# The last expert of a mixture of experts: its order of work and the split of its last columns

## The chip, the core and the metric

The kernel runs on one core of a Trainium2 chip. The metric is the device time of one execution in microseconds (us). The engines are TensorE (PE in the rows, PEld its weight loads), VectorE (DVE), ScalarE (ACT), GpSimd (POOL) and SyncE (SP). Each works through its own instructions in program order; they meet through semaphores. Weights come from HBM by DMA, issued from SP.

## What is computed

Two transformer blocks run over 256 tokens of width 1024. The change lies in the last part of the second block, a mixture of 32 experts with top-4 routing, and in the final norm behind it:

```python
def expert_block(args):
    xb, e = args
    u = xb @ w1[e] + b1[e]                                  # first product
    glu = jnp.minimum(u[:, ::2], SWIGLU_LIMIT)
    lin = jnp.clip(u[:, 1::2], -SWIGLU_LIMIT, SWIGLU_LIMIT)
    a = glu * jax.nn.sigmoid(SWIGLU_ALPHA * glu) * (lin + 1.0)
    return a @ w2[e] + b2[e]                                # second product
...
y = jnp.zeros((T + 1, D), jnp.float32).at[row_tok].add(yb * row_gate[:, None])
...
x = x + gt_f[:, None, :] * moe(...)
return rms_norm(x, g_final)
```

`w1[e]` is 1024 x 2048 and `w2[e]` 1024 x 1024, all in float32.

## The kernel before

**Dense dispatch.** Every expert has room for 64 tokens. Expert e gathers its tokens by a matmul with a one-hot matrix (`xe`), and its result goes back to the 256 tokens, weighted by the gates, by a matmul with another one-hot matrix (`gT`). Tokens beyond 64 for one expert are treated by the loop under `tc.If(items > 0)` at the end.

**The stream of weights.** `seq` lists the weight tiles in the order in which they are loaded and used. Each is 1 MB (128 x 2048 floats). `(1, e, k)`, k = 0 to 7, are rows 128k to 128k+127 of `w1[e]`; `(2, e, k)`, k = 0 to 3, are each two blocks of 128 rows of `w2[e]`. The order is: the eight tiles of the first product of e, then the four tiles of the second product of e - 1. `mload` issues the loads on SP, mostly two tiles (2 MB) in one DMA, into a ring of R = 22 tile places. The four tiles of expert 31's second product come from an array of their own, `w_mlp2_last`, in five issues: three of 1 MB and, for the fourth tile, two of 512 KB.

**The loop over experts.** For expert e and each k: `up_k` multiplies one tile of the first product (line 1280, into the PSUM tile `u`). After k = 1 and k = 2 it takes one `step` each of the `combine` of expert e - 2: per step four matmuls into two PSUM tiles `cp` (line 1331) and two additions to the sum `macc` on VectorE (line 1334). After k = 5 it prepares expert e - 1: `turn` transposes its activations on TensorE (`ap`, line 1298) and copies them back on ScalarE (`aT`, line 1300); VectorE builds the gate matrix `gp` (line 1303), TensorE transposes it (`gq`, line 1306) and VectorE copies it (`gT`, line 1308). After k = 7 come `up_bias` (line 1274) and `glu`, a chain VectorE, VectorE, ScalarE, VectorE, VectorE (lines 1285 to 1291). Then `second` multiplies the four tiles of expert e - 1's second product (line 1314), adds its bias (line 1318) and multiplies by the gain (`ys`, line 1320). It does not need the `glu` of e, so TensorE has work while that chain runs.

**The end.** For e = 31, `final_gain` (line 1394) spreads the last norm's gain over the partitions after k = 4. After half of expert 30's second product, `last_start` puts the bias into expert 31's PSUM tiles (line 1362) and copies its gain rows on VectorE (`gl`, line 1364), and `turn` prepares expert 31. Behind the loop come the rest of expert 30's second product, the steps of its combine and expert 31's tiles (`last_tile`, line 1373). Those give the output columns in halves: tiles 0 and 1 make columns 0 to 511, tiles 2 and 3 columns 512 to 1023. After tile 3 both halves are combined (lines 1383 and 1386). Sums of squares (line 1492), square root (1505), reciprocal (1506), products with the gain (1500, 1510, 1512) and four stores on SP (1511, 1513) follow. PSUM tiles of the pool `pm` rotate through four places, those of `pu` (`u`, and at the end `pe`) through two.

Of the kernel before, what the change touches and what calls it, by code (L numbers as in the profile page):

```python
# [20 lines left out]
P = 128  # L21
# [21 lines left out]
def tile_two_blocks(ctx, tc, A, out, dbg=None):  # L43
# [999 lines left out]
    for e in range(NE):  # L1043
        seq += [(1, e, k) for k in range(KT)]
        if e > 0:
            seq += [(2, e - 1, k) for k in range(4)]
# [247 lines left out]
    def turn(a, cols, own=None):  # L1294
# [5 lines left out]
        nc.scalar.copy(aT, ap)  # L1300
        gp = mt.tile([P, 2, P], F32, tag="one", name="gp", bufs=1)
# [7 lines left out]
        return aT, gT  # L1309
# [34 lines left out]
    def turned(a, e, own=None):  # L1344
        return turn(a, [(rk[:, t, e:e + 1], gate[:, t, e:e + 1]) for t in range(2)], own)
# [11 lines left out]
    def last_start():  # L1357

        gl = lw[0][:, D:].rearrange("p (h n) -> p h n", h=2)
        y = [pm.tile([P, 512], F32, tag="pm", name="y") for _ in range(2)]  # L1360
        for hf in range(2):
            mm(y[hf][0:64], sel_of(NE - 1), bsp[:, 2048 + hf * 512:2048 + (hf + 1) * 512], start=True, stop=False)
            for g in range(2):
                nc.vector.tensor_copy(gl[64 * g:64 * g + 64, hf, :], gtf[64 * hf:64 * hf + 64, :])
        return y, gl

    def last_tile(k2, y, aT):
        z = take(2, NE - 1, k2)
        for kk in range(4):
            k = k2 % 2 * 4 + kk  # L1370
            g = slice(64 * (k % 2), 64 * (k % 2) + 64)
            a = aT[:, k % 4 * P + 64 * (k // 4):k % 4 * P + 64 * (k // 4) + 64]
            mm(y[k2 // 2][g], a, z[:, kk * 512:(kk + 1) * 512], start=k == 1, stop=k >= 6)  # L1373

    def last_rows(hf, y, gl):
        ys = lw[2][:, D + hf * 512:D + (hf + 1) * 512]
        nc.vector.tensor_mul(ys, y[hf], gl[:, hf, :])
        return ys

    def last_combine(hf, ys, gT):  # L1380
        cp = [(pb, pa)[hf][:, t * 512:(t + 1) * 512] for t in range(2)]
        for t in range(2):
            mm(cp[t], gT[:, t * P:(t + 1) * P], ys, start=True, stop=True)  # L1383
        for t in range(2):
            d = macc[:, t, hf * 512:(hf + 1) * 512]
# [13 lines left out]
    lw = []  # L1399
    a, comb, tab, gth, aT = None, None, items_table(), None, None  # L1400
    for e in range(NE):
# [5 lines left out]
        for k in range(KT):  # L1407
# [5 lines left out]
            if k in (1, 2):  # L1413
                step(comb)
            if k == 5 and e > 0:
                sec = second(e - 1, *turned(a, e - 1))
            if e == 0 and k >= 4:
                step(tab)
# [23 lines left out]
    last_tile(2, y31, aT31)  # L1442
# [44 lines left out]
    halves = [slice(hf * 512, (hf + 1) * 512) for hf in range(2)]  # L1487
    junk = lw[7][:, 0:512]
    fg = [lw[1][:, :D], lw[1][:, D:]]

    def squares(t, hf):
        act(junk, macc[:, t, halves[hf]], AF.Square, accum_out=fs[:, t, hf:hf + 1])  # L1492

    last_tile(3, y31, aT31)
    ys31.append(last_rows(1, y31, gl))
    last_combine(0, ys31[0], gT31)
    last_combine(1, ys31[1], gT31)
    for t in range(2):
        squares(t, 0)
        nc.gpsimd.tensor_mul(fg[t][:, :512], macc[:, t, :512], gfin[:, :512])  # L1500

    def factor(t):
        f = fs[:, t, 3:4]
        nc.vector.tensor_add(f, fs[:, t, 0:1], fs[:, t, 1:2])  # L1504
        act(f, f, AF.Sqrt, bias=eps, scale=1.0 / D)  # L1505
        nc.vector.reciprocal(f, f)  # L1506
        return f

    def store(t, f):
        stt(fg[t][:, 512:], macc[:, t, 512:], f, gfin[:, 512:], op0=ALU.mult, op1=ALU.mult)  # L1510
        nc.sync.dma_start(ov[:, t, 512:], fg[t][:, 512:])
        nc.scalar.mul(fg[t][:, :512], fg[t][:, :512], f)  # L1512
        nc.sync.dma_start(ov[:, t, :512], fg[t][:, :512])

    squares(0, 1)
    f = factor(0)
    squares(1, 1)
    store(0, f)
    store(1, factor(1))


# [56 lines left out]
def layout(inp):  # L1578
# [20 lines left out]
    o["w_mlp2_last"] = np.ascontiguousarray(w2[31].reshape(2, 4, P, 2, 512).transpose(3, 0, 2, 1, 4)).reshape(4, P, W)  # L1599
# [21 lines left out]
```

## Time and profile before

| what | us |
|---|---|
| runs of the kernel before | 1790.49, 1792.51, 1793.85 |
| their median | 1792.51 |
| the profiled execution | 1793.98 |
| its span, first to last instruction | 1791.8 |
| TensorE busy in it | 1722.1 (96%) |
| DMA, mean over the span | 319 GB/s |

The profiled execution is 1.47 us above the median, and 2.2 us of it lie outside the span. All times of rows are counted from the span's start. A busy TensorE is not TensorE at its peak: the end of a matmul is modelled. Rows of the timeline merge like instructions: "x16" are 16 of them, and one float32 matmul of the code shows as two.

### The profile page before, as it was taken

How to read it: one execution, taken by the hardware profiler on the slowest of the kernel's cores; microseconds unless marked ns; L12 is line 12 of the kernel's file. 1: busy time of each engine (PE TensorE's matmuls, PEld its weight loads, DVE VectorE, ACT ScalarE, POOL GpSimd, SP SyncE). 2: the span in 40 equal slices, each digit the busy share in tenths (PEclk: the TensorE clock that was granted, in tenths of full speed). 3: DMA queues.
4: the chain of work that ended last, by engine and by line, in shares of the span. 5: the costliest groups of instructions: out<-in, count | busy, mean ns of one | idle time of the engine just before them, and what ended most of it. 6: DMA issues, size and time to landing. Idle time of an engine off the chain costs nothing. (4 is left out here: it accounts for less than half of the span.)

```text
span 1791.8 us, 25574 instructions
## 1 busy us (share of the span) xinstructions
PE 1722.1 (96%) x10942; PEld 1143.3 (64%) x10942; DVE 871.6 (49%) x1330; ACT 484.7 (27%) x754; POOL 120.0 (7%) x132
## 2 busy tenths in 40 slices
PE   8999999999999999999999999999999999999987
PEld 7999989999998999999633333333333333333322
DVE  7767777776778667766322222222222222222223
ACT  4545564544445544454200000000000000000001
POOL 2100022321012000000000000000000000000000
PEclk8999999999999999999999999999999999999999
DMA  6556556568656654566899999999999999999995
GB/s 224 175 181 218 186 172 207 191 226 310 244 201 223 223 206 151 200 233 258 351 429 428 431 428 432 430 428 430 431 428 432 428 430 428 432 428 430 430 428 224
DMA packets 67899, 571.79 MB, mean 319 GB/s; under 512 B 8526, under 2 KB 13574, under 8 KB 23622
## 3 DMA queue, kind: packets, MB, share of 16 engines
q1 hardware_dynamic: 56400, 538.45, 74.1%
q0 software_dynamic: 7904, 28.08, 4.6%
q10 hardware_dynamic: 3478, 3.59, 0.6%
q8 instruction: 87, 1.43, 0.3%
q14 instruction: 30, 0.25, 0.0%
HBM read 568.44 MB, written 4.02 MB: 319 GB/s over the span
## 5 line engine op out<-in xcount | busy, mean ns | idle before, releaser
L1280 PE MATMUL u<-mw,hx 128*64 128x512 f32 x2048 | 472.8, 600 | 19.2 <-DMA mw<-in_w_mlp_dram 18.1
L114 DVE TENSOR_TENSOR hl<-w,hl 128x1024 fp32r<-128x1024 f32 (+1 forms) x256 | 317.0, 1253 | 154.0 <-ACT hl L113 153.2
L1280 PEld LDWEIGHTS u<-mw,hx 128*64 128x64 f32 x2048 | 135.4, 136 | 293.8 <-issue 244.1
L113 ACT ACTIVATE hl<-w 128x1024 fp32r<-128x1024 f32 (+1 forms) x256 | 260.0, 1032 | 129.1 <-PE ps L222 77.4
L1314 PE MATMUL y<-mw,aT 128*64 128x512 f32 x992 | 224.3, 601 | 19.1 <-DMA mw<-in_w_mlp_dram 19.1
L1314 PEld LDWEIGHTS y<-mw,aT 128*64 128x64 f32 x992 | 72.0, 138 | 154.2 <-issue 126.8
L1334 DVE TENSOR_TENSOR macc<-macc,cp 128x512 f32<-128x512 f32 x124 | 79.7, 684 | 179.1 <-PE cp L1331 179.1
L220 PE MATMUL ps<-xnh,hl 128*128 128x256 f32 (+1 forms) x512 | 152.8, 298 | 2.9 <-ACT hl L113 2.9
L222 PE MATMUL ps<-xnh,hl 128*128 128x256 f32 (+1 forms) x512 | 148.7, 290 | 5.0 <-DVE hl L114 5.0
L221 PE MATMUL ps<-xnl,hl 128*128 128x256 f32 (+1 forms) x512 | 147.7, 289 | 0.0
L1300 ACT COPY aT<-ap 128x512 f32<-128x512 f32 x31 | 18.2, 586 | 413.7 <-PE ap L1298 413.7
L220 PE MATMUL ps<-h,hl 128*128 128x256 f32 x384 | 110.2, 287 | 0.0
L221 PE MATMUL ps<-h,hl 128*128 128x256 f32 x384 | 108.8, 283 | 1.2 <-DVE h L114 1.2
L222 PE MATMUL ps<-h,hl 128*128 128x256 f32 x384 | 108.6, 283 | 0.0
L220 PEld LDWEIGHTS ps<-xnh,hl 128*128 128x128 f32 x512 | 98.8, 193 | 7.6 <-ACT hl L113 4.1
L222 PEld LDWEIGHTS ps<-xnh,hl 128*128 128x128 f32 x512 | 98.6, 193 | 6.1 <-DVE hl L114 5.9
L222 PE MATMUL ps<-hnh,hl 128*128 128x256 f32 x352 | 99.8, 284 | 1.0 <-DVE hl L114 1.0
L220 PE MATMUL ps<-hnh,hl 128*128 128x256 f32 x352 | 99.8, 284 | 0.0
L221 PE MATMUL ps<-hnl,hl 128*128 128x256 f32 x352 | 99.6, 283 | 0.0
L221 PEld LDWEIGHTS ps<-xnl,hl 128*128 128x128 f32 x512 | 98.6, 193 | 0.1
L1320 DVE TENSOR_TENSOR ys<-y,m 128x512 f32<-128x512 f32 x31 | 21.4, 692 | 134.3 <-PE y L1318 134.3
L1308 DVE COPY m<-gq 128x256 f32<-128x256 f32 x31 | 13.2, 425 | 140.5 <-PE gq L1306 140.5
(458 smaller groups left out, 2904.5 us busy)
## 6 DMA issues: line engine op xcount, KB each, us to landing
mw<-in_w_mlp_dram SPq DMA_DIRECT2D x156, 2048.0 KB, 31.5
mw<-in_w_mlp_dram SPq DMA_DIRECT2D x68, 1024.0 KB, 31.2
w<-in_w_in_dram SPq DMA_DIRECT2D x60, 1024.0 KB, 4.9
wa<-in_w_ada_dram POOLq DMA_DIRECT2D x48, 512.0 KB, 4.8
w<-in_w_ffn_gate_dram SPq DMA_DIRECT2D x11, 1024.0 KB, 5.3
w<-in_w_ffn_up_dram SPq DMA_DIRECT2D x11, 1024.0 KB, 4.7
w<-in_w_gate_dram SPq DMA_DIRECT2D x8, 1024.0 KB, 4.8
w<-in_w_ffn_down_dram SPq DMA_DIRECT2D x8, 1024.0 KB, 5.3
```

Source lines behind the costliest of these rows:

```text
L113: act(hi, src, AF.Copy)
L114: (eng or nc.vector).tensor_sub(lo, src, hi.bitcast(F32))
L220: mm(ps[m], hi[:, k, cs], xh[:, k0 + k, r], start=first, stop=False, skip_group_check=True)
L221: mm(ps[m], hi[:, k, cs], xl[:, k0 + k, r], start=False, stop=False, skip_group_check=True)
L222: mm(ps[m], lo[:, k, cs], xh[:, k0 + k, r], start=False, stop=last, skip_group_check=True)
L1280: mm(u[64 * hf:64 * hf + 64, c * 512:(c + 1) * 512], xk, wcol(hf, c), start=k == 0, stop=False)
L1300: nc.scalar.copy(aT, ap)
L1308: nc.vector.tensor_copy(gT, gq[:, :256])
L1314: mm(y[64 * hf:64 * hf + 64, :], a, wcol(hf), start=k == 0, stop=False)
L1320: nc.vector.tensor_mul(ys, y, gtf)
L1334: nc.vector.tensor_add(d, d, cp[hf])
```

## The change

The order of tiles is changed for the last expert alone: the four tiles of expert 30's second product stand behind the first four tiles of expert 31's first product. In the loop of e = 31, after k = 3, both steps of expert 29's combine are taken, then `turn` and the whole second product of expert 30. Its combine takes its steps after k = 5 and k = 6. `last_start` and the gate half of `turn` (`turn_gates`) come after k = 6. After `glu` of expert 31 only the other half (`turn_rows`) is left ahead of its tiles.

The columns of expert 31's second product come in a half and two quarters (`cols3`): tiles 0 and 1 still make columns 0 to 511; tile 2 makes 512 to 767 and tile 3 makes 768 to 1023, each with all eight row blocks. The halves and quarters are combined as they come; the first two run ahead of and inside tile 3. Squares, products with the gain, and stores follow this split. Two of the four stores go to ScalarE's queue.

```diff
-        seq += [(1, e, k) for k in range(KT)]
-        if e > 0:
-            seq += [(2, e - 1, k) for k in range(4)]
+        first = [(1, e, k) for k in range(KT)]
+        prior = [(2, e - 1, k) for k in range(4)] if e > 0 else []
+        seq += first + prior if e < NE - 1 else first[:4] + prior + first[4:]
...
     def last_start():
         gl = lw[0][:, D:].rearrange("p (h n) -> p h n", h=2)
-        y = [pm.tile([P, 512], F32, tag="pm", name="y") for _ in range(2)]
+        y = [pm.tile([P, c.stop - c.start], F32, tag="pm", name="y") for c in cols3]
         for hf in range(2):
-            mm(y[hf][0:64], sel_of(NE - 1), bsp[:, 2048 + hf * 512:2048 + (hf + 1) * 512], start=True, stop=False)
             for g in range(2):
                 nc.vector.tensor_copy(gl[64 * g:64 * g + 64, hf, :], gtf[64 * hf:64 * hf + 64, :])
+        for q, c in enumerate(cols3):
+            mm(y[q][0:64], sel_of(NE - 1), bsp[:, 2048 + c.start:2048 + c.stop], start=True, stop=False)
...
-    lw = []
+    lw, cols3 = [], (slice(0, 512), slice(512, 768), slice(768, 1024))
...
-            if k in (1, 2):
+            if k in ((5, 6) if last else (1, 2)):
                 step(comb)
-            if k == 5 and e > 0:
+            if k == (3 if last else 5) and e > 0:
+                if last:
+                    step(comb)
+                    step(comb)
                 sec = second(e - 1, *turned(a, e - 1))
+                if last:
+                    finish(sec)
+                    comb = st["comb"]
...
             if last and k == 4:
                 gfin = final_gain()
+            if last and k == 6:
+                finish(comb)
+                y31, gl = last_start()
+                pa = pu.tile([P, 1024], F32, tag="u", name="pe")
+                own31 = lw[2][:, 0:512], lw[2][:, 512:768], pa[:, 0:512], pa[:, 512:768]
+                gT31 = turn_gates(gates_of(e), own31)
         up_bias(u, sel_of(e))
         a = glu(u)
         if last:
-            pa, pb = (pu.tile([P, 1024], F32, tag="u", name="pe") for _ in range(2))
-        for k2, _ in enumerate(sec if e > 0 else ()):
-            if last and k2 == 1:
-                last = last_start()
-                aT = turned(a, e, (lw[2][:, 0:512], lw[2][:, 512:768], pa[:, 0:512], pa[:, 512:768]))
-        comb = st.get("comb")
-    aT31, gT31 = aT
-    y31, gl = last
-    step(comb)
-    last_tile(0, y31, aT31)
-    step(comb)
-    last_tile(1, y31, aT31)
+            aT31 = turn_rows(a, own31)
+            pb = pu.tile([P, 1024], F32, tag="u", name="pe")
+        elif e > 0:
+            finish(sec)
+            comb = st["comb"]
+    for k2 in range(2):
+        finish(last_tile(k2, y31, aT31))
...
+    end = last_tile(3, y31, aT31)
+    last_combine(0, ys31[0], gT31, [pb[:, t * 512:(t + 1) * 512] for t in range(2)])
     for t in range(2):
         squares(t, 0)
+        gained(t, 0)
+    next(end)
+    cq = pm.tile([P, 2, 256], F32, tag="pm", name="cq")
+    last_combine(1, ys31[1], gT31, [cq[:, t, :] for t in range(2)])
+    for t in range(2):
+        squares(t, 1)
+        gained(t, 1)
+    finish(end)
+    ys31.append(last_rows(2, y31, gl))
+    last_combine(2, ys31[2], gT31, [pa[:, t * 512:t * 512 + 256] for t in range(2)])
...
+    nc.gpsimd.tensor_add(part[:, :, 0], fs[:, :, 0], fs[:, :, 1])
+    nc.gpsimd.tensor_scalar(part[:, :, 1], part[:, :, 0], 1.0 / D, EPS, op0=ALU.mult, op1=ALU.add)
+    squares(0, 2)
+    nc.vector.tensor_tensor_reduce(out=junk2[:, :256], in0=macc[:, 1, c], in1=macc[:, 1, c], scale=1.0, scalar=0.0,
+                                   op0=ALU.mult, op1=ALU.add, accum_out=fs[:, 1, 2:3])
+    for t in range(2):
         f = fs[:, t, 3:4]
+        act(f, fs[:, t, 2:3], AF.Sqrt, bias=part[:, t, 1:2], scale=1.0 / D)
         nc.vector.reciprocal(f, f)
+        nc.scalar.mul(fg[t][:, 0:512], fg[t][:, 0:512], f)
+        nc.scalar.dma_start(ov[:, t, 0:512], fg[t][:, 0:512])
+        stt(fg[t][:, 768:], macc[:, t, 768:], f, gfin[:, 768:], op0=ALU.mult, op1=ALU.mult)
+        nc.vector.tensor_scalar_mul(fg[t][:, 512:768], fg[t][:, 512:768], f)
         nc.sync.dma_start(ov[:, t, 512:], fg[t][:, 512:])
```

`turn` is split into `turn_rows` and `turn_gates` without other changes, `last_tile` becomes a generator that yields after its fourth row block, and the host packs the last two tiles of `w_mlp2_last` as quarters.

## Rows read from the trace of the kernel before

**Rows 1.** The page: GB/s of all DMA, 40 slices of the span.

```profile
GB/s 224 175 181 218 186 172 207 191 226 310 244 201 223 223 206 151 200 233 258 351 429 428 431 428 432 430 428 430 431 428 432 428 430 428 432 428 430 430 428 224
```

**Rows 2.** PE's waits from 700 us on: total us, times, longest.

```profile
PE y L1314 <- DMA mw<-in_w_mlp_dram: 19.1, 17, 2.2
PE u L1280 <- DMA mw<-in_w_mlp_dram: 18.1, 25, 2.4
```

**Rows 3.** Timeline of SP's issues: start, us, engine, line.

```profile
1726.64 0.33 SPq L1078 DMA_DIRECT2D mw<-in_w_mlp_dram  x1
...
1729.36 0.33 SPq L1078 DMA_DIRECT2D mw<-in_w_mlp_dram  x1
...
1748.53 0.33 SPq L1075 DMA_DIRECT2D mw<-in_w_mlp_last_dram  x1
```

**Rows 4.** DMA view of those three windows: KB, us from issue to landing.

```profile
mw<-in_w_mlp_dram SPq DMA_DIRECT2D x1, 2048.0 KB, 31.5
...
mw<-in_w_mlp_dram SPq DMA_DIRECT2D x1, 2048.0 KB, 33.7
...
mw<-in_w_mlp_last_dram SPq DMA_DIRECT2D x1, 512.0 KB, 24.4
```

**Rows 5.** Timeline, 1733 to 1759 us: start, us, engine, line, [idle before].

```profile
1733.88 5.35 PE L1314 MATMUL y<-mw,aT 128*64 128x512 f32 x16 [2.24 <-DMA mw<-in_w_mlp_dram]
...
1739.28 3.60 PE L1280 MATMUL u<-mw,hx 128*64 128x512 f32 x16
...
1742.82 1.13 PE L1331 MATMUL cp<-ys,m 64*128 64x512 f32 x4
...
1743.88 1.94 PE L1280 MATMUL u<-mw,hx 128*64 128x512 f32 x8
...
1743.98 1.29 DVE L1334 TENSOR_TENSOR macc<-macc,cp 128x512 f32<-128x512 f32 x2 [3.79 <-PE cp L1331]
...
1750.39 1.98 PE L1394 MATMUL ps<-mw,ones 128*128 128x512 f32 x4
...
1754.97 3.65 PE L1280 MATMUL u<-mw,hx 128*64 128x512 f32 x16
```

**Rows 6.** Timeline, 1758 to 1769 us.

```profile
1758.46 0.60 PE L1274 MATMUL u<-bsp,sel 96*64 96x512 bf16 x4
...
1759.10 0.70 DVE L1285 TENSOR_SCALAR u<-u 128x512 f32<-128x512 f32 x1 [3.60 <-PE u L1274]
...
1762.61 1.74 DVE L1364 COPY mw<-m 64x512 f32<-64x512 f32 x4
...
1762.86 0.65 PE L1298 MATMUL pe<-ident,lin 128*128 128x128 f32 x4
...
1763.55 0.59 ACT L1300 COPY mw<-pe 128x512 f32<-128x512 f32 x1 [2.31 <-PE pe L1298]
1764.37 0.60 DVE L1303 TENSOR_SCALAR gp<-m,macc,lg 128x128 f32<-128x128 f32 x2
...
1765.29 3.65 PE L1314 MATMUL y<-mw,aT 128*64 128x512 f32 x16
```

**Rows 7.** Timeline, 1771 us to the end.

```profile
1771.01 1.94 PE L1373 MATMUL y<-mw 128*64 128x512 f32 x8
...
1779.61 3.70 PE L1383 MATMUL pe<-mw 128*128 128x512 f32 x8
...
1787.08 0.72 ACT L1512 ACTIVATE mw<-mw,fs 128x512 f32<-128x512 f32 x1 [0.29 <-DVE fs L1506]
...
1788.22 0.41 SPq L1513 DMA_DIRECT2D out_dram<-mw  x1
```

**Rows 8.** Windows: busy PE, PEld, DVE, ACT, POOL, then granted clock, DMA share.

```profile
1734.60:1738.00 3.40, 3.40 (x10) 0.96 (x8) 0.00 (x0) 0.00 (x0) 0.00 (x0) 0.50 1.02 434
1783.40:1785.80 2.40, 0.00 (x0) 0.00 (x0) 1.75 (x5) 1.88 (x6) 1.57 (x2) 1.00 0.01 3
1785.80:1791.80 6.00, 0.00 (x0) 0.00 (x0) 1.54 (x4) 1.71 (x5) 0.00 (x0) 0.50 0.45 175
```

More of the change, by code (lines that the diff above doesn't have):

```diff
@@ L1292, in glu, with turn_rows @@
         return l
-    def turn(a, cols, own=None):
+    def turn_rows(a, own=None):
         ap = own[2] if own else pm.tile([P, 512], F32, tag="pm", name="ap")
@@ L1300, in turn, with turn_gates @@
         nc.scalar.copy(aT, ap)
+        return aT
+    def turn_gates(cols, own=None):
         gp = mt.tile([P, 2, P], F32, tag="one", name="gp", bufs=1)
@@ L1308, in turn @@
         nc.vector.tensor_copy(gT, gq[:, :256])
-        return aT, gT
+        return gT
+    def turn(a, cols, own=None):
+        return turn_rows(a, own), turn_gates(cols, own)
     def down_k(y, aT, wcol, k):
@@ L1342, in step, with gates_of, turned @@
             next(g, None)
-    def turned(a, e, own=None):
-        return turn(a, [(rk[:, t, e:e + 1], gate[:, t, e:e + 1]) for t in range(2)], own)
+    def gates_of(e):
+        return [(rk[:, t, e:e + 1], gate[:, t, e:e + 1]) for t in range(2)]
+    def turned(a, e):
+        return turn(a, gates_of(e))
     def second(e, aT, gT):
@@ L1359, in last_start, with last_rows, last_combine @@
         gl = lw[0][:, D:].rearrange("p (h n) -> p h n", h=2)
-        y = [pm.tile([P, 512], F32, tag="pm", name="y") for _ in range(2)]
+        y = [pm.tile([P, c.stop - c.start], F32, tag="pm", name="y") for c in cols3]
         for hf in range(2):
-            mm(y[hf][0:64], sel_of(NE - 1), bsp[:, 2048 + hf * 512:2048 + (hf + 1) * 512], start=True, stop=False)
             for g in range(2):
                 nc.vector.tensor_copy(gl[64 * g:64 * g + 64, hf, :], gtf[64 * hf:64 * hf + 64, :])
-        return y, gl
+        for q, c in enumerate(cols3):
+            mm(y[q][0:64], sel_of(NE - 1), bsp[:, 2048 + c.start:2048 + c.stop], start=True, stop=False)
+        return y, gl.rearrange("p h n -> p (h n)")
     def last_tile(k2, y, aT):
         z = take(2, NE - 1, k2)
-        for kk in range(4):
-            k = k2 % 2 * 4 + kk
+        q, ks = (0, range(4 * k2, 4 * k2 + 4)) if k2 < 2 else (k2 - 1, range(KT))
+        n = cols3[q].stop - cols3[q].start
+        for kk, k in enumerate(ks):
             g = slice(64 * (k % 2), 64 * (k % 2) + 64)
             a = aT[:, k % 4 * P + 64 * (k // 4):k % 4 * P + 64 * (k // 4) + 64]
[L1373 to L1377, printed above, removed]
-        return ys
-    def last_combine(hf, ys, gT):
-        cp = [(pb, pa)[hf][:, t * 512:(t + 1) * 512] for t in range(2)]
+            mm(y[q][g], a, z[:, kk * n:(kk + 1) * n], start=k == 1, stop=k >= 6)
+            if kk == 3:
+                yield
+    def last_rows(q, y, gl):
+        ys = lw[2][:, D:][:, cols3[q]]
+        nc.vector.tensor_mul(ys, y[q], gl[:, cols3[q]])
+        return ys
+    def last_combine(q, ys, gT, cp):
         for t in range(2):
@@ L1384, in last_combine @@
         for t in range(2):
-            d = macc[:, t, hf * 512:(hf + 1) * 512]
+            d = macc[:, t, cols3[q]]
             nc.vector.tensor_add(d, d, cp[t])
@@ L1486, in tile_two_blocks, with squares @@
     fs = cst.tile([P, 2, 4], F32, name="fs")
-    halves = [slice(hf * 512, (hf + 1) * 512) for hf in range(2)]
+    part = cst.tile([P, 2, 2], F32, name="part")
     junk = lw[7][:, 0:512]
+    junk2 = lw[7][:, 512:1024]
     fg = [lw[1][:, :D], lw[1][:, D:]]
[L1491 to L1497, printed above, removed]
+    def squares(t, q):
+        c = cols3[q]
+        act(junk[:, :c.stop - c.start], macc[:, t, c], AF.Square, accum_out=fs[:, t, q:q + 1])
@@ L1498, in tile_two_blocks, with gained @@
+    def gained(t, q):
+        nc.gpsimd.tensor_mul(fg[t][:, cols3[q]], macc[:, t, cols3[q]], gfin[:, cols3[q]])
+    end = last_tile(3, y31, aT31)
+    last_combine(0, ys31[0], gT31, [pb[:, t * 512:(t + 1) * 512] for t in range(2)])
     for t in range(2):
         squares(t, 0)
-        nc.gpsimd.tensor_mul(fg[t][:, :512], macc[:, t, :512], gfin[:, :512])
-    def factor(t):
+        gained(t, 0)
+    next(end)
+    cq = pm.tile([P, 2, 256], F32, tag="pm", name="cq")
+    last_combine(1, ys31[1], gT31, [cq[:, t, :] for t in range(2)])
@@ L1511, in store @@
         nc.sync.dma_start(ov[:, t, 512:], fg[t][:, 512:])
[L1512 to L1519, printed above, removed]
 def constants():
@@ L1597, in layout @@
     o["w_mlp2_2"] = np.ascontiguousarray(w2.reshape(32, 2, 4, P, D).transpose(0, 1, 3, 2, 4)).reshape(32, 2, P, 4 * D)
-    o["w_mlp2_last"] = np.ascontiguousarray(w2[31].reshape(2, 4, P, 2, 512).transpose(3, 0, 2, 1, 4)).reshape(4, P, W)
+    halves = w2[31][:, :512].reshape(2, 4, P, 512).transpose(0, 2, 1, 3)
+    quarters = w2[31][:, 512:].reshape(8, P, 2, 256).transpose(2, 1, 0, 3)
+    o["w_mlp2_last"] = np.concatenate([halves.reshape(2, P, W), quarters.reshape(2, P, W)], axis=0)
     b12 = np.concatenate([a["b_mlp1_2"].reshape(32, 2 * D), a["b_mlp2_2"].reshape(32, D)], axis=1)
```

9 lines of the change are left out of this document (3 added, 6 removed).

## Prediction

> **What bounds the kernel now.** I read the page first, then who TensorE waits for, then the loads with their landings, then the timeline of the last 60 us. The page shows the stream of expert weights at some 430 GB/s from the middle of the span on [rows 1]. In that stretch TensorE waits for little but landing weights: 42 waits, 37.2 us in all, none over 2.4 us [rows 2]. So up to the last expert the stream sets the pace. The question is who sets it at the end. The reader is to see two things there.
>
> First, the places in the stream. A tile's landing is its issue plus the time to landing. The last two 2 MB issues are expert 30's second product: 1726.64 + 31.5 = 1758.1 and 1729.36 + 33.7 = 1763.1. The last half tile of expert 31 lands at 1748.53 + 24.4 = 1772.9 [rows 3, 4]. Second, TensorE is late by then: it begins expert 31's first last tile at 1771.0, needs no wait for a landing up to the last one, and ends the four tiles at 1779.6, 6.7 us after the last landing [rows 7]. So from about 1750 on the order of TensorE's own work and its waits for other engines set the end, and the stream doesn't.
>
> **What the change does to the stream.** Same bytes, same issues, same ring; only what stands in a place differs. Expert 30's four tiles move forward by four places, and tiles 4 to 7 of the first product move into the two issues above: tiles 4 and 5 land at 1758.1, tiles 6 and 7 at 1763.1. Before, tiles 6 and 7 were taken up at 1754.97 [rows 5]. SP's issues wait for earlier landings, not for the moved work, so I cost the new order at nothing on SP; were it not so, TensorE would be later still.
>
> **The chain, step by step.** Durations: two tiles take 1758.46 − 1754.97 = 3.49, one 1.75 [rows 5, 6]; one step of a combine 1743.88 − 1742.82 = 1.06 [rows 5].
> - Tiles 0 to 3 without combine steps: 1739.28 + 4 × 1.75 = 1746.3.
> - Both steps of combine 29 follow, to 1748.4. VectorE starts its additions 1743.98 − 1742.82 = 1.16 after the first matmul and needs 2 × 1.29, then 0.60 for the gate matrix [rows 5, 6]: 1746.3 + 1.16 + 2.58 + 0.60 = 1750.6. The gate transposes wait for it. They stand ahead of expert 30's second product on TensorE, which starts 0.32 after `gp` ends, as at 1764.97 to 1765.29 [rows 6]: 1750.9. With the first transposes ended at 1748.4 + 0.65, this is a wait of some 1.5 us that the kernel before did not have here, as it took the steps two tiles earlier.
> - Four tiles, 2 × 3.49, and the bias, about 0.4: 1758.3. Tile 4 has landed just then. Tile 4, `final_gain` at 1.98 less the usual overlap (1.9), tile 5: 1758.3 + 1.75 + 1.9 + 1.75 = 1763.7. A step of combine 30, tile 6, the second step: 1763.7 + 1.06 + 1.75 + 1.06 = 1767.6. Tile 6 landed before that, at 1763.1.
> - Here the change adds its worst wait. VectorE adds the second step (1767.6 + 0.1 + 1.29 = 1769.0), then copies the gain rows for 1.74 and builds `gp` for 0.60 [rows 6]: 1771.3. TensorE has three small bias matmuls for that time. Behind the waiting transposes stand tile 7, `up_bias` and the whole `glu`. Tile 7 starts at 1771.7. The bound from below is what the kernel before shows for the same pair: transposes of 0.65 from 1762.86, next tile 0.32 behind `gp`, a wait of 1.4 [rows 6]. I take 2.7, because there the copies started early and here they queue behind additions that are released late.
> - Tile 7 to 1773.5. From `up_bias` to the first last tile I read the path of before: to `glu`'s start 1759.10 − 1758.46 = 0.64; to the transposes 1762.86 − 1759.10 = 3.76; to the end of the copy of `aT` 1763.55 + 0.59 − 1762.86 = 1.28 [rows 6]; in sum 5.7. In the kernel before expert 30's tiles ran beside that chain; that cover is gone, and TensorE stands idle for some 4 us. The first last tile starts at 1779.2, against 1771.0 [rows 7]: 8.2 later.
> - Three tiles 5.2, the branch 0.4, first combine 1.7 (half of the 3.70 of rows 7, with overlap), the last tile 1.7, the second combine 0.9 and changes between them 0.2: 1789.3. All tiles have landed at 1772.9, so the finer split of the columns wins nothing against the stream. The product with the gain on a quarter (0.5) and two small matmuls (0.9 and 0.3 until seen): 1791.0 for the last result. Before, it was 1779.61 + 3.70 = 1783.3 [rows 7]: 7.7 later.
> - From the last result to the end it was 1791.8 − 1783.3 = 8.5. Now: addition on a quarter 0.4, square 0.5, root and reciprocal 0.5, the product of 0.72, its store's issue on ScalarE's queue 0.4 (as on SP, rows 7), ahead of which the second token block's root now waits, then root, reciprocal and product 1.5: 4.0. From the last issue to the end is 1791.8 − 1788.22 = 3.6. In sum 7.6, a gain of 0.9. The first two pieces' squares and GpSimd's products lie beside the last tile. Two operations that the trace does not show, a product-and-sum on VectorE and two tiny GpSimd sums, are off this path if they stay under 0.7 each, and cost up to 1 if not.
>
> The sum without the clock: 7.7 − 0.9 = +6.8.
>
> **The clock.** TensorE waited 2.24 us, and behind that the granted clock was 0.50, which is 1.2 GHz, for a stretch [rows 5, 8]: the sixteen matmuls took 5.35 instead of 3.60, a price of 1.75. Behind the wait of 1.4 the sixteen took 3.65: none [rows 6]. The idle 4 us in `glu` should bring a fall, 1.7 on the last tiles. The wait of 2.7 at the gates may bring one too, 0 to 1.7; I take 1.1, since part of the slow stretch would lie in `glu`. In sum 2.8.
>
> The Trainium skill says in "TensorE: Matmul & The Clock Gate", "Loop structure matters more than you think", that VectorE's copying of a result does not break the engine's warmth, while a long wait for a DMA does. By that rule these two waits would cost no clock, and the time would be +6.8. The trace speaks against it: with VectorE, ScalarE and GpSimd at work and a DMA share of 0.01, TensorE's idle 2.4 us at the end was followed by 0.50 [rows 8]. It is a rival below.
>
> **The sum.** 6.8 + 2.8 = +9.6 on the profiled execution: 1793.98 becomes 1803.6. That execution lies 1.47 above the median, so the median goes from 1792.51 to 1802.1; I say 1802.
>
> **Rivals.** A change of 0.2%, 3.6 us, is about what a measurement can tell from none.
> - No fall of the clock: +6.8, 1799.3. For it: the wait of 1.4 without a fall. Against it: the longer waits above. 0.18.
> - The wait at the gates is hidden, as `gp` for expert 30 was in the kernel before: 2.7 and its clock less, +5.8, 1798.3. For it: only VectorE's order decides. Against it: the copies stand behind the last additions. 0.15.
> - Not slower: the stream, not TensorE, paces the last expert. Then tile 6 starts at its landing, 1763.1. With tiles 6 and 7 (3.5), one step (1.1), bias and gates (0.8) and the 5.7 of `glu` the last tiles start at 1774.2, 3.2 later, and the end is 3.2 − 0.5 − 0.9 = +1.8, 1794.3. It decides for "not slower" where the last tiles start by 1776.0, and for a gain only where they start before 1772.4; tiles 6 and 7 and `glu` alone end at 1772.3, with the combine and the gates out of the way. Against it: by the sum above TensorE comes to tile 6 at 1764.8, 1.7 after its landing, and the gates hold it 2.7 more. 0.11, of which 0.04 for faster.
> - The slow clock holds through most of the last tiles, 3.4 more: 1805.5. 0.04.
>
> **How the numbers follow.** The forecast has 0.52. All but the third rival are slower by more than 0.2%: 0.89; same 0.07, faster 0.04. The range leaves out the third rival (0.11) and the last one's end: 1796.5, which is the hidden wait without any fall (+4.1), to 1805, the sum with both falls in full and a late GpSimd (6.8 + 3.4 + 1 = +11.2, 1803.7) and part of the way to the last rival.
>
> **What would show it.** Right: loads land at the same times; TensorE idle for VectorE's `gp` twice, some 1.5 and 2.7 us, and some 4 us between `up_bias` and the transposes, with a granted clock of 0.50 behind; last tiles from 1779 to 1782 on; from the last matmul to the end a little under 8 us. Wrong: tiles 6 and 7 of the first product taken up well before 1763, or last tiles begun before 1776.0.

## The result, and the profile after

The changed kernel took 1813.5 us (median; 1813.24 to 1814.74) beside 1793.18 us for the kernel before (1790.49 to 1794.2). The ratio is 1.0117, with a 95% interval from 1.0105 to 1.0129: 20.3 us slower, where +9.6 was forecast. The sign was right. The time lies beyond the upper end of the range. The profiled execution took 1813.45 us and its span 1811.7 us, 19.9 more than before.

What TensorE waits for, from 700 us on, with total us, times and longest wait, in the kernel after (to set beside [rows 2]):

```profile
PE y L1321 <- DMA mw<-in_w_mlp_dram: 23.0, 17, 2.5
PE u L1280 <- DMA mw<-in_w_mlp_dram: 22.0, 29, 2.5
PE pe L1298 <- DVE lin L1291: 3.7, 1, 3.7
PE pe L1310 <- DVE gp L1307: 2.3, 1, 2.3
PE gq L1310 <- DVE gp L1307: 1.4, 1, 1.4
PE pe L1397 <- DVEq L1468: 1.1, 1, 1.1
```

The last four rows are the waits that the change makes, forecast as 4, 2.7, 1.5 and 0.4: all are there, and the last is larger. The first two rows are the surprise. They answer to 19.1 and 18.1 before: TensorE waits 7.8 us more for landing weights, 6.0 of it up to expert 31's first tile, in a stretch whose order of work the change leaves as it was. The page has a clue. Its row of GB/s in 40 slices, in the kernel after (beside [rows 1]):

```profile
GB/s 222 178 173 227 175 171 219 195 239 287 252 189 239 224 185 160 192 244 258 405 426 425 425 427 423 427 426 425 424 427 425 427 425 426 425 426 426 426 424 107
```

From the middle of the span on the stream moves 423 to 427 GB/s, where it was 428 to 432. So TensorE comes late to the last expert. Its timeline from shortly before that to the end, in the kernel after (start, us, engine, line, operation, and in brackets the idle time before):

```profile
1739.41 3.65 PE L1321 MATMUL y<-mw,aT 128*64 128x512 f32 x16 [2.46 <-DMA mw<-in_w_mlp_dram]
...
1744.21 7.09 PE L1280 MATMUL u<-mw,hx 128*64 128x512 f32 x32 [0.92 <-DMA mw<-in_w_mlp_dram]
...
1755.18 0.58 PE L1310 MATMUL gq<-ident,gp 128*128 128x128 f32 x2 [1.38 <-DVE gp L1307]
1755.70 3.65 PE L1321 MATMUL y<-mw,aT 128*64 128x512 f32 x16
...
1765.01 1.94 PE L1280 MATMUL u<-mw,hx 128*64 128x512 f32 x8 [1.03 <-DMA mw<-in_w_mlp_dram]
...
1778.10 0.58 PE L1310 MATMUL pe<-ident,gp 128*128 128x128 f32 x2 [2.35 <-DVE gp L1307]
1778.62 3.61 PE L1280 MATMUL u<-mw,hx 128*64 128x512 f32 x8
...
1786.36 1.11 PE L1298 MATMUL pe<-ident,lin 128*128 128x128 f32 x4 [3.68 <-DVE lin L1291]
1788.15 7.46 PE L1386 MATMUL y<-mw 128*64 128x512 f32 x32 [0.68 <-ACT mw L1300]
1796.70 1.96 PE L1397 MATMUL pe<-mw 128*128 128x512 f32 x4 [1.08 <-DVEq L1468]
...
1802.27 1.13 PE L1397 MATMUL pe<-mw 128*128 128x256 f32 x4 [0.53 <-DVE mw L1392]
```

Expert 31's first product begins at 1744.21; before, it began at 1739.28 [rows 5]. Two durations show a slow clock. A tile (x8) took 3.61 us behind the wait of 2.35, where one took 1.94 at 1765.01; and the first three of expert 31's last tiles (x32, since the third has twice as many matmuls of half the columns) took 7.46. The windows view of those stretches, in the kernel after (its length, busy us of PE, PEld, DVE, ACT and POOL, then granted clock, DMA share and GB/s):

```profile
1778.70:1782.10 3.40, 3.40 (x10) 0.91 (x12) 0.42 (x1) 0.00 (x0) 0.00 (x0) 0.50 0.02 7
1785.60:1792.40 6.80, 5.36 (x14) 1.94 (x16) 0.69 (x1) 1.87 (x2) 0.00 (x0) 0.50 0.01 2
1792.40:1800.00 7.60, 6.52 (x38) 2.95 (x35) 2.40 (x4) 0.59 (x2) 0.48 (x1) 1.00 0.01 2
```

The granted clock is 0.50, which is 1.2 GHz, behind both long waits for VectorE, and full again from 1792.4 to 1800. It was not so behind every wait of that length: after the 2.46 us of the first row of this timeline sixteen matmuls took 3.65, the time at full clock.

### The profile page after: what moved, and what is told of

Its sections match the earlier page's. It is cut to its first block, busy times and chain, and to the rows that moved or that the text cites. A ratio compares the mean times of both kernels' runs of the same rounds, so it can differ in the third digit from the quotient of the medians.

```text
span 1811.7 us, 25638 instructions
## 1 busy us (share of the span) xinstructions
PE 1728.0 (95%) x10963; PEld 1146.6 (63%) x10963; DVE 872.3 (48%) x1335; ACT 485.1 (27%) x756; POOL 121.2 (7%) x136
## 5 line engine op out<-in xcount | busy, mean ns | idle before, releaser
L1285 DVE TENSOR_SCALAR u<-u 128x512 f32<-128x512 f32 x32 | 22.4, 700 | 120.6 <-PE u L1274 120.6
```

What stands on the lines that cost most here:

```text
L1285: nc.vector.tensor_scalar_min(g, g, 7.0)
```

## The experiments

### Did the stream become slower by where its tiles lie?

The bytes and the issues are the same, so I compared the addresses that the two programs were given. The change allocates one tile more, `part`, in the pool `cst`: 16 bytes per partition. That pool is opened before all others on its side of the SBUF, and everything allocated there behind it moves by 32 bytes. Before, 15 of the ring's 22 tile places begin on a multiple of 256 bytes; after, none does. **Theory**: the addresses alone slow the stream. **Rival**: the new order of tiles does.

**before_shift**: the kernel before, with a tile of that size in the same pool and nothing else.

```diff
     fs = cst.tile([P, 2, 4], F32, name="fs")
+    pad = cst.tile([P, 4], F32, name="pad")
```

> The kernel before with one unused tile of 16 bytes per partition (32 with rounding) beside fs, so that every tile behind it, 15 of the 22 ring places among them, lies 32 bytes further, as in the changed kernel. Places theory (the stream lost speed because ring places that began on multiples of 256 bytes no longer do): the last landing comes some 7 us later and the time grows by 5 to 8 us, to 1798 to 1801. Rival (the new order of the last expert or chance made the stream slower): no change, within 1.5 us of 1793.

1800.94 us (1800.07 to 1804.54) beside 1792.47; ratio 1.0054 [1.004, 1.0068]. A tile that nobody reads costs 8.5 us.

**after_home**: the change, with `part` in spare floats beside another tile's, so that all addresses are as before.

```diff
-    gneps = cst.tile([P, 1], F32, name="gneps")
+    gneps8 = cst.tile([P, 8], F32, name="gneps")
+    gneps = gneps8[:, 0:1]
...
-    part = cst.tile([P, 2, 2], F32, name="part")
+    part = gneps8[:, 4:8].rearrange("p (t j) -> p t j", t=2)
```

> The changed kernel with its new tile part put into the free floats of the tile of gneps, so that all addresses are those of the kernel before. Places theory: the stream is as fast as before, last landing about 1773, and the time falls by 5 to 8 us, to 1805 to 1808, which leaves +12 to +15 for order and waits. Rival: stays at 1813 to 1815.

1805.08 us (1801.98 to 1805.73); ratio 1.0072 [1.0058, 1.0086]. So of the 20.3 us some 8 are the addresses, seen from either side, and 12.6 are the new order and the new end. The windows view of the steady stream in four kernels, columns as above; the last is GB/s. The kernel before:

```profile
1200.00:1650.00 450.00, 420.24 (x2024) 152.54 (x2022) 115.45 (x206) 23.03 (x39) 0.00 (x0) 0.99 1.01 430
```

The kernel after:

```profile
1200.00:1650.00 450.00, 417.03 (x2000) 150.76 (x1998) 115.34 (x206) 22.80 (x39) 0.00 (x0) 0.99 1.01 426
```

before_shift:

```profile
1200.00:1650.00 450.00, 415.15 (x1994) 149.90 (x1990) 114.94 (x205) 22.45 (x38) 0.00 (x0) 0.99 1.01 426
```

after_home:

```profile
1200.00:1650.00 450.00, 418.28 (x2023) 152.27 (x2020) 116.06 (x208) 22.43 (x38) 0.00 (x0) 1.00 1.01 430
```

430 or 426 goes with the addresses, not with the order of the tiles. The steady stream fills 19 of the page's slices, some 850 us; 4/430 of that is 7.9 us, about the price. The single packets show it too: of those of 16 KB in that stretch 98.5% took 611 or 612 ns in the kernel before, and 8.7% in the kernel after, where most took 614 to 621.

### Which addresses, and how many of them?

**before_aligned**: the seven places of the kernel before that lie off a multiple of 256 are moved onto one. Three small tiles of the loop under `tc.If` go into a weight tile that is free by then, and a pad of 224 bytes stands on the other side.

```diff
+        pools["edge"] = ctx.enter_context(tc.tile_pool(name="edge", bufs=1, side="right"))
+        pools["edge"].tile([P, 56], F32, name="edge")
...
-            off = mt.tile([P, 1], F32, tag="xoff", name="off", bufs=1)
+            off = lw[6][:, 1288:1289]
```

> The kernel before with the seven ring places that do not begin on a multiple of 256 bytes moved onto one (three small tiles of the overflow loop put into a used weight tile, 224 bytes left free at the upper end). Places theory: seven places gain what fifteen lost, so the stream ends some 3 us earlier and the time falls by 2 to 4 us, to 1789 to 1791. Rival: no change.

1792.1 us; ratio 0.9998 [0.9989, 1.0007]. No gain: this expectation missed. The seven places cost nothing as long as the other fifteen lie well, so what a place costs isn't its own alone.

**shift224** and **shift64**: the kernel before, everything on the lower side moved by 224 bytes (56 floats, below) or by 64 (16 floats) instead of 32. The small tiles under `tc.If` stand in a weight tile as in before_aligned.

```diff
     fs = cst.tile([P, 2, 4], F32, name="fs")
+    pad = cst.tile([P, 56], F32, name="pad")
```

> The kernel before with all places on the lower side moved by 224 bytes, so that all 22 begin 224 bytes past a multiple of 256 (before: 15 at 0, 5 at 224, 2 at 192; in the changed kernel 15 at 32, 7 at 224). If any place off a multiple of 256 costs once most of them are off: packets of 16 KB at 614 to 621 ns, 425 GB/s, 1800. If it is the 32 bytes past a multiple that cost: 611 ns, 429 GB/s, 1791 to 1794.

> The kernel before with the lower side moved by 64 bytes: 17 ring places begin 64 bytes past a multiple of 256, 5 at 224 as before. If beginning on a multiple of 256 is what counts: 425 GB/s, 1800 to 1803 as in before_shift and shift224. If a multiple of 64 is enough: 429 GB/s, 1791 to 1794.

1802.46 us; ratio 1.0061 [1.0045, 1.0076], and 1800.79 us; ratio 1.0046 [1.003, 1.0061]. All three offsets cost about the same, and both kernels show 426 GB/s. So the size of the offset makes little difference, and a multiple of 64 is not enough. 128 was not tried.

**low32** and **mt32**: 32 bytes are put in at a later place, so that less moves. In low32 they stand behind the pool `big`, and 12 of the 22 places lie off. In mt32 they stand ahead of the pool `mt` alone: the experts' working tiles move, and seven places lie off as before.

```diff
+    gap = ctx.enter_context(tc.tile_pool(name="gap", bufs=1))
+    gap.tile([P, 4], F32, name="gap")
```

> The kernel before with 32 bytes put between the ten ring places of the pool big and those behind it: 12 of 22 places are off a multiple of 256 (before: 7, before_shift: 22), while the token rows, macc and the rest of the pool big stay where they were. If the places off a multiple add up against a limit that 7 do not reach: between the two, 426.5 to 428 GB/s, 1794 to 1798. If something in the pool big other than weight places made the stream slow: 429 GB/s, 1791 to 1794.

> The kernel before with 32 bytes put ahead of the pool mt alone: the working tiles of the expert loop (bias parts, sigmoid, activations, gate matrix) and the last ring places (192 to 224 past a multiple of 256) move, the number of ring places off a multiple of 256 stays 7. If the weight places make the stream slow: 429 GB/s, packets at 611 ns. If moved working tiles do (they moved in low32, shift64, shift224, before_shift and the changed kernel, too): 427.6 GB/s or less, as in low32. The time counts only if the stage begins as early as before; the rate of the stream decides.

mt32: 1792.96 us; ratio 1.0004 [0.9995, 1.0014], so the working tiles aren't it. low32: 1808.77 us; ratio 1.0088 [1.0073, 1.0104], beyond both of the ranges that were expected. That total says nothing on the question, since the kernel lost some 12 us ahead of the steady stream, as its page's row of GB/s shows:

```profile
GB/s 222 176 177 219 184 170 221 188 229 292 256 199 234 206 198 168 187 234 233 297 428 428 430 428 429 428 427 428 429 428 429 428 428 427 431 428 429 428 427 227
```

The twentieth slice has 297, where [rows 1] has 351. Why I didn't look into. Its steady rate does count:

| kernel | places off a multiple of 256, of 22 | GB/s, 1200 to 1650 us | 16 KB packets of 611 or 612 ns |
|---|---|---|---|
| before_aligned | 0 | 430 | 99.8% |
| before | 7 | 430 | 98.5% |
| mt32 | 7 | 430 | 98.5% |
| low32 | 12 | 428 | 66% |
| shift64 | 22 | 426 | 13.5% |
| before_shift | 22 | 426 | 8.6% |
| after | 22 | 426 | 8.7% |
| shift224 | 22 | 426 | 5.9% |

In these kernels the rate is lower with more places off, beginning somewhere between 7 and 12. How many and which ones go together here, and the single packets say that it matters which. I put them to places by their order in the stream, an estimate good to about one place; `big`, `mra` to `mre`, `mrs` and `mrt` are the pools that hold the ring's places. In low32 the slow packets lie mostly in `mrc` and `mrd`, whose places moved by 32 (in three of the four only 4% to 14% took 611 or 612 ns), and in the two of `mrb`, which did not move (31% and 42%; 93% and 94% in the kernel before). Five places of `big` and the first of `mra` have 98% or more there. In the kernel after, `mra` and `mrb`, at the addresses of before, are as slow as the rest (5% to 14%). So, by this estimate, what a place costs hangs on its own address and on those of others.

The Trainium skill says in "DMA: Bandwidth & Descriptors", "How a descriptor splits into AXI transactions", that a descriptor which does not start on a multiple of 256 bytes gets a first transaction from the boundary below it, whose bytes ahead of the start are fetched and not used. It tells this of reading, and here the places that are written moved. That 64 isn't enough, by these runs, agrees with 256 as the unit; that seven places off cost nothing does not follow from it. What inside the transfers binds stays open, and so does whether the other tiles of `big`, which move in four of these kernels, have a part in it.

### What do the two waits in the middle cost, and the clock behind them?

These kernels start from after_home. **Theory**: the second gate wait, the uncovered `glu` and the slow clock behind hold most of its 12.6 us. The medians of these kernels come with intervals of 2 to 2.5 us either way, so the traces are set beside them. In all five the fifth tile of expert 31 waits for its landing, and from its start to the end of the last result the work is the same but for the edits:

| kernel | over the kernel before beside it, medians, us | fifth tile to last result, profiled execution, us |
|---|---|---|
| after_home | 12.6 | 37.7 |
| gates_early | 8.1 | 34.2 |
| glu_busy | 10.2 | 35.8 |
| both | 6.0 | 31.3 |
| no_glu_wait | 2.5 | 28.9 |

Two rows of TensorE's timeline in after_home, the transposes behind the wait for `glu` and the last tiles:

```profile
1775.24 1.12 PE L1299 MATMUL pe<-ident,lin 128*128 128x128 f32 x4 [3.68 <-DVE lin L1292]
...
1777.03 7.16 PE L1387 MATMUL y<-mw 128*64 128x512 f32 x32 [0.67 <-ACT mw L1301]
```

**gates_early**: the gate matrix and its transposes are taken at k = 4, ahead of `final_gain`, so that VectorE builds `gp` before the copies and additions queue up.

```diff
             if last and k == 4:
+                pa = pu.tile([P, 1024], F32, tag="u", name="pe")
+                own31 = lw[2][:, 0:512], lw[2][:, 512:768], pa[:, 0:512], pa[:, 512:768]
+                gT31 = turn_gates(gates_of(e), own31)
                 gfin = final_gain()
             if last and k == 6:
                 finish(comb)
                 y31, gl = last_start()
-                pa = pu.tile([P, 1024], F32, tag="u", name="pe")
-                own31 = lw[2][:, 0:512], lw[2][:, 512:768], pa[:, 0:512], pa[:, 512:768]
-                gT31 = turn_gates(gates_of(e), own31)
```

> The changed kernel at the old addresses (after_home, 1805.1), with expert 31's gate matrix built, transposed and copied after k = 4, ahead of final_gain, instead of after k = 6; the gain rows are copied after k = 6 as before. My theory: the 2.35 us in which TensorE waits for gp behind VectorE's additions and copies go, and with them the slow clock of tile 7 (3.10 instead of 1.94): 3.5 us less, 1801 to 1802. Rival (something else holds tile 7, or the copies now hold glu): under 1 us less.

1800.35 us; ratio 1.0048 [1.0034, 1.0062]. Set beside the kernel before each time, that is 4.5 less than after_home by the medians, and 3.5 by the traces. The second gate wait and the slow clock behind it are both gone; the timeline of TensorE, in gates_early:

```profile
1766.60 1.98 PE L1281 MATMUL u<-mw,hx 128*64 128x512 f32 x8
...
1774.26 8.12 PE L1387 MATMUL y<-mw 128*64 128x512 f32 x32 [0.67 <-ACT mw L1301]
```

The last tile of the first product takes 1.98. The slow clock behind `glu` is still there, in 8.12 for the last tiles.

**glu_busy**: four matmuls, whose result nobody uses, fill TensorE's idle time in `glu`.

```diff
+        if last:
+            idle = pm.tile([P, 512], F32, tag="pm", name="idle")
+            for _ in range(4):
+                mm(idle, ones, lw[1][:, 0:512], start=True, stop=True)
         a = glu(u)
```

> The changed kernel at the old addresses (after_home) with four matmuls of 128 x 512 behind up_bias into an unused PSUM tile, so that TensorE has 3.4 us of work while glu runs; their result is not used. If TensorE's idleness brings the fall of the clock: transposes and last tiles run at full clock, 7.16 becomes some 5.2 and 1.12 becomes 0.65, 2 to 2.5 us less, 1802.5 to 1803.2. Rival (the fall comes anyway, or the extra matmuls hold the transposes): 0 to 1 us more.

1802.42 us; ratio 1.0058 [1.0044, 1.0071], with no step of the kernel taken out. By the medians that is 2.4 less than after_home, which their noise doesn't tell from nothing; the traces show where it comes from. The timeline of TensorE, in glu_busy:

```profile
1776.90 3.70 PE L1457 MATMUL idle<-mw,ones 128*128 128x512 f32 x8
1780.65 0.65 PE L1299 MATMUL pe<-ident,lin 128*128 128x128 f32 x4
1781.98 5.38 PE L1387 MATMUL y<-mw 128*64 128x512 f32 x32 [0.68 <-ACT mw L1301]
```

5.38 for the last tiles and 0.65 for the transposes, instead of 7.16 and 1.12 in after_home. The price of the clock behind the `glu` wait is thus measured by itself: (7.16 − 5.38) + (1.12 − 0.65) = 2.3. (The whole stretch is only 1.9 shorter, since in this execution the slow clock behind the second gate wait held the eighth tile for 3.63 instead of 3.10.) TensorE's idleness brings that fall: VectorE and ScalarE do the same `glu` in both kernels.

**both**: the two edits together.

> Both edits together. If they are separate costs, 5.5 to 6.5 us less than after_home, 1798.5 to 1799.6, which leaves +6 to +7 over the kernel before: the 4 us of glu without useful work, the first wait for gp, and the late tiles. If the falls of the clock are one and the same, less than 4.5.

1798.29 us; ratio 1.0034 [1.0022, 1.0046]. That is 6.6 less than after_home by the medians, 6.4 by the traces, and still 6.0 more than the kernel before. Its clock stays at 1.00; windows view of both, columns as above:

```profile
1769.70:1776.00 6.30, 5.57 (x20) 2.34 (x20) 2.77 (x4) 2.11 (x3) 0.00 (x0) 1.00 0.04 14
1776.00:1788.00 12.00, 10.39 (x56) 4.73 (x52) 3.58 (x7) 2.83 (x9) 3.83 (x4) 1.00 0.01 2
```

**no_glu_wait**: gates_early, with expert 31's transposes reading a weight tile that landed long ago in place of `glu`'s result. Its product doesn't contain expert 31's activations.

```diff
-            aT31 = turn_rows(a, own31)
+            aT31 = turn_rows(lw[1][:, 0:512], own31)
```

> gates_early (1800.4) with expert 31's activations left out of the way: the transposes read a weight tile that has long landed instead of glu's result, so expert 31's contribution is not the reference's; glu itself still runs. If the uncovered glu is what is left of the loss: TensorE goes on behind up_bias, the 3.7 us of waiting and the slow clock behind it (8.12 instead of 5.4) go, 6 to 6.5 us less, 1794 to 1794.5. If the last tiles then wait for something else (landings, the gain rows): under 4 us less.

1795.45 us; ratio 1.0019 [1.0009, 1.0029]: 5.6 less than gates_early by the medians and 5.3 by the traces, where 6 to 6.5 were expected. The timeline of TensorE, in no_glu_wait:

```profile
1768.87 0.66 PE L1299 MATMUL pe<-ident,mw 128*128 128x128 f32 x4
1771.66 5.38 PE L1387 MATMUL y<-mw 128*64 128x512 f32 x32 [2.13 <-ACTq L1469]
```

The wait of 3.7 is gone, and ahead of the last tiles 2.13 stand in place of 0.67. The copy of `aT` is ScalarE's, and there it is queued behind `glu`'s sigmoid, which waits for VectorE; the timeline of ScalarE, in no_glu_wait:

```profile
1770.53 0.60 ACT L1290 ACTIVATE sig<-u 128x512 f32<-128x512 f32 x1 [10.01 <-DVE lin L1288]
1771.02 0.58 ACT L1301 COPY mw<-pe 128x512 f32<-128x512 f32 x1
```

A wait that was taken away on one engine was still there in the program order of the next.

### What is the finer split worth alone?

**tail_only**: the order of tiles of the kernel before, with the half, the two quarters and the new end, and with the addresses of before. Expert 30's combine, which comes late in this order, writes into `pb` here. Two lines of its diff:

```diff
+    lw, cols3 = [], (slice(0, 512), slice(512, 768), slice(768, 1024))
...
-    halves = [slice(hf * 512, (hf + 1) * 512) for hf in range(2)]
```

> The order of the kernel before with the half and two quarters and the new end, at the addresses of the kernel before. My sum has 0.5 to 1.4 us of gain in the end and no clock fall: 1791.5 to 1793. Rival (the pieces cost more than they save: the branch, change-overs, three small tiles): 1793.5 to 1795.

1793.52 us; ratio 1.0004 [0.9995, 1.0013]: no gain. The 0.5 to 1.4 of my own sum did not come; the time stands at the lower end of the rival's range. The timeline of TensorE, in tail_only:

```profile
1756.77 0.60 PE L1275 MATMUL u<-bsp,sel 96*64 96x512 bf16 x4
...
1776.89 1.98 PE L1398 MATMUL pe<-mw 128*128 128x512 f32 x4 [0.98 <-DVEq L1462]
...
1782.49 1.13 PE L1398 MATMUL pe<-mw 128*128 128x256 f32 x4 [0.53 <-DVE mw L1393]
```

From `up_bias` to the last result it is 1782.49 + 1.13 − 1756.77 = 26.9 us; before it was 1783.3 − 1758.46 = 24.8 [rows 6, 7]. TensorE loses 2.0: 0.98 at the branch (0.16 before), 0.53 for the product on a quarter, and the rest in changes between the pieces. Behind the last result 0.4 is won, 8.1 instead of 8.5.

### What the kernel before still had

**before_gates**: the kernel before, with expert 31's gate matrix taken between its seventh and eighth tile. The gate wait of 1.4 in that kernel goes. It is the first of these two rows of TensorE's timeline, in the kernel before; the second is the wait that the next experiment takes up:

```profile
1764.87 0.49 PE L1306 MATMUL pe<-ident,gp 128*128 128x128 f32 x2 [1.36 <-DVE gp L1303]
...
1769.95 1.13 PE L1331 MATMUL cp<-ys,m 64*128 64x512 f32 x4 [0.79 <-DVE ys L1320]
```

```diff
+            if last and k == 6:
+                pa = pu.tile([P, 1024], F32, tag="u", name="pe")
+                own31 = lw[2][:, 0:512], lw[2][:, 512:768], pa[:, 0:512], pa[:, 512:768]
+                gT31 = turn_gates(gates_of(e), own31)
```

> The kernel before with one edit of its own: expert 31's gate matrix is built and transposed after k = 6 of its first product instead of in the middle of expert 30's second product, where TensorE waits 1.36 us for it. If that wait is on the path: 1 to 1.4 us less, 1790.9 to 1791.5. If TensorE is given the time back as a wait elsewhere: no change.

1791.83 us; ratio 0.9994 [0.9985, 1.0003]: 1.1 less, as expected, and within what can be told from no change.

**before_best**: beside that, expert 31's first last tile ahead of both steps of expert 30's combine, so that VectorE's product `ys` gets cover.

```diff
-    step(comb)
     last_tile(0, y31, aT31)
     step(comb)
     last_tile(1, y31, aT31)
+    step(comb)
```

> before_gates (1791.8, 1.1 under the kernel before) with expert 31's first last tile ahead of the first step of expert 30's combine instead of behind it, so that TensorE does not wait 0.79 us for ys there. If both waits were on the path: 1.7 to 2.2 us under the kernel before, 1790.3 to 1791.2. If the time comes back as a wait elsewhere: as before_gates.

1789.12 us (1786.79 to 1792.78) beside 1792.99; ratio 0.9978 [0.9969, 0.9987]: 3.9 less than the kernel before, and faster than both kernels. The timeline of TensorE, in before_best:

```profile
1761.38 3.65 PE L1321 MATMUL y<-mw,aT 128*64 128x512 f32 x16
...
1765.08 1.89 PE L1383 MATMUL y<-mw 128*64 128x512 f32 x8
1766.90 1.13 PE L1338 MATMUL cp<-ys,m 64*128 64x512 f32 x4
```

No row has a wait in brackets, where the kernel before had 1.4 and 0.8. These two make 2.2 of the 3.9. From the seventh tile of expert 31 to the last result it is 26.2 us in this trace and 28.3 in the kernel before, which is just these 2.2. By its interval the gain may be as small as 0.0013 of the time, 2.3 us, so nothing shows that more than the two waits went.

## Why the prediction missed, step by step

The sum compares spans: forecast +9.6 (6.8 and 2.8 for the clock), measured +19.9.

**The stream, "nothing on SP": wrong, 6.7 us.** This is the step that failed. I argued that the same bytes, issues and ring give the same landings. The same ring isn't the same addresses. The new order itself does cost the stream nothing (after_home, 430 GB/s). But the change allocates `part`, and I priced only the work of GpSimd on it. The last half tile's issue, from the timeline of SP in the kernel after:

```profile
1755.22 0.33 SPq L1075 DMA_DIRECT2D mw<-in_w_mlp_last_dram  x1
```

And from its DMA view, KB and us from issue to landing:

```profile
mw<-in_w_mlp_last_dram SPq DMA_DIRECT2D x1, 512.0 KB, 24.7
```

It landed at 1779.9, where 1772.9 was forecast [rows 3, 4]: 7.0 later, 6.7 of it by the issue and not by the transfer. On TensorE it is 1744.21 − 1739.28 = 4.9 at the start of expert 31, and 1.8 more until its fifth tile, which waited for its landing (started 1765.01; forecast 1758.3 + 4.9 = 1763.2). This sets one execution against another: in executions with the addresses of before, expert 31's first tile starts at 1734.8 to 1739.3. before_shift and after_home give 8.5 and 7.7 for the addresses by the medians, each beside its own runs of the kernel before.

**The chain's waits: right.** Set off by those 4.9, expert 30's second product was due at 1750.9 + 4.9 = 1755.8 and started at 1755.70. The first gate wait was 1.38 (forecast 1.5), the second 2.35 (2.7), the idle time in `glu` 3.68 and 0.68 more for the copy of `aT` (forecast 4 in all). From the fifth tile to the eighth it came out within 0.2: due at 1771.7 − 1758.3 = 13.4 behind the fifth, and started 13.6 behind it.

**The clock: the fall came, its size was too small by 1.6.** I forecast 1.7 on the last tiles, and 1.1 at the gates as a middle between nothing and 1.7. Measured against the chain: 3.61 − 1.94 = 1.67 on the eighth tile, 1.11 − 0.66 = 0.45 on the transposes and 7.46 − 5.2 = 2.26 on the last tiles, in sum 4.4 instead of 2.8. Against the rows of glu_busy the part behind `glu` is (7.46 − 5.38) + (1.11 − 0.65) = 2.5. I had assumed that the two slow stretches share time. They don't: each wait was followed by its own, at 0.50. The rival without a fall is out, and so is the one that hides the second gate wait. I had the rule from one case, the 2.24 us in the kernel before [rows 5], and it is weaker than I took it for. At that same place in the program, in front of the second half of expert 29's second product, a wait of 2.46 in the kernel after and of 2.24 in after_home was followed by 3.65, at full clock; in before_best 2.24 was followed by 5.35. Both long waits of the new order brought a fall in every trace here in which TensorE stood idle in them, but the length of a wait alone does not decide. The Trainium skill says in "TensorE: Matmul & The Clock Gate", "Loop structure matters more than you think", that VectorE's copying doesn't break the engine's warmth where the next matmuls follow at once. I read that as a rule for any wait for VectorE, and that was too wide: TensorE waited 2.35 and 3.68 us here, and 0.50 came behind both. In glu_busy VectorE does the same work, TensorE isn't idle, and the last tiles run at full clock in 5.38, which agrees with the sentence.

**The last tiles and the end: short by 1.8.** The branch wait was 1.08 instead of 0.4: the trace has TensorE released there by VectorE, which has the product with the gain ahead of its own branch: 0.7. The wait for the product on a quarter and the changes between pieces took 0.4 more than I gave them. And from the last result, 1803.4, to the end it was 8.3 and not 7.6: 0.7. The timeline of the kernel after, with the two operations that the trace of before did not show, and with ScalarE's store:

```profile
1803.36 0.18 POOL L1536 TENSOR_TENSOR part<-fs 128x2 f32<-128x2 f32 x1
...
1804.30 0.42 DVE L1540 CUSTOM_DVE_ANT_0 mw<-macc 128x256 f32<-128x256 f32 x1
...
1805.90 0.38 ACTq L1547 DMA_DIRECT2D out_dram<-mw  x1
...
1806.33 0.29 ACT L1544 ACTIVATE fs<-fs,part 128x1 f32<-128x1 f32 x1 [0.46 <-ACT mw L1546]
```

GpSimd's sums and the product-and-sum stayed off the path, as assumed, at 0.18 and 0.42. The second token block's square root stands on ScalarE behind the first one's product and behind its store's issue of 0.38, as forecast. Up to the last issue of a store it was 1807.64 − 1803.40 = 4.2 (forecast 4.0), and from there to the end of the span 4.0, where the kernel before has 3.6; why that last part was longer stays open.

In sum 6.7 + 0.2 + 1.6 + 1.8 = 10.3 on top of the forecast's 9.6: 19.9. Some two thirds of the miss are the addresses. Without them the prediction would have been short by 3, and after_home's 1805.08 lies just above the range's upper end.

**What the change was worth by itself.** In `both`, without either clock fall and without the second gate wait, +6.0 is left. Its trace shows most of what that is. From expert 31's first tile to the last result it is 44.0 us in the kernel before and 51.5 in `both`. In that stretch of `both` TensorE has 8.9 us of waits and of work that nobody uses: `glu` (3.7), the first gate wait (1.4), landings (1.2), the branch (1.1), the copy of `aT` (0.7), the product on a quarter (0.5) and a wait of 0.3 for VectorE. In the kernel before it has 2.3 (1.36, 0.79 and 0.16). The difference of 6.6 is most of the 7.4; the rest I leave open, and by the medians, within their noise, the whole is 6.0. In the kernel before, half of expert 30's second product lay beside the chain of `glu` and `aT`. Taking it away from there is the largest part of the cost, 4.4, and the finer split, which was to meet late landings, met a TensorE that came after them.

## What to carry to other kernels

Before costing a change to a kernel that is bound by a stream, compare the addresses of the tiles it writes: a small tile in an early pool moves everything that is allocated behind it on its side. Work that covers a chain over VectorE and ScalarE is worth more where it stands than ahead of it; count for each chain what TensorE still has to do, and price the slow clock behind each long wait that this leaves open, as a chance and not as a certainty. An early place for the gate matrix, ahead of VectorE's copies, was the part that could be kept.

## What the hardware showed that I had not expected

- A shift of 32, 64 or 224 bytes of the weight tiles costs the stream 0.9% (430 to 426 GB/s), and it isn't a cost of single places: 7 of 22 off a multiple of 256 cost nothing, 12 cost about half (428). Which places they are has a part in it, too.
- Behind a wait of TensorE for VectorE of 2.35 us the granted clock was 0.50, and behind one of 1.38 it was not. But behind the 2.13 us in no_glu_wait the last tiles took 5.38, at full clock, and behind 2.46 us for a landing in the kernel after sixteen matmuls took 3.65, while 2.24 us in the kernel before were followed by 0.50 [rows 5, 8]: the length of the wait alone doesn't decide, and these runs don't tell what does. Matmuls whose result nobody reads, in the idle time, gave 2.3 us of slow clock back (glu_busy beside after_home), and 3.0 in `both` beside gates_early.
- The price of the fall is not fixed by the wait: behind the same idle time in `glu` (3.68 or 3.69) the last tiles took 7.16 us in after_home and 8.12 in gates_early, where the tile ahead of it had run at full clock, in 1.98.
